# RMSNorm and matrix product: input held in two buffers of sixteen tiles instead of five of eight

## The chip, the cores and the metric

The kernel runs on one core of one Trainium2 chip. The metric is the device time of one execution in microseconds (us); "before" and "changed" below are always compared over runs on the same chip, interleaved in rounds. Times of one kernel mostly agree within some 0.5% from run to run.

## The reference

```python
batch, seq, dim, out_dim = 16, 1024, 512, 768        # x: 16384 rows of 512, float32
rms = np.sqrt(np.mean(x ** 2, axis=-1, keepdims=True) + eps)
x_norm = x / rms * gamma
return np.matmul(x_norm, weight).astype(np.float32)  # 16384 rows of 768, float32
```

The rows form 128 tiles of 128 rows. A tile of x is 256 KB, a tile of the output 384 KB; with the weights 85.5 MB must cross between memory and the core.

## The kernel before

For each pair of tiles: GpSimd casts x to bf16 (into one of four small buffers), TensorE transposes the cast tiles by words, VectorE copies the transposes out of PSUM, TensorE multiplies with the weights, ScalarE computes the squares' sums, and ScalarE (even tiles) and VectorE (odd tiles) scale the product by 1/rms into the output buffer. All loads and stores are issued by the sync engine, on one DMA queue, in program order; a load or store that must wait for its buffer or its data holds back everything behind it.

```python
G = 8
AHEAD = 28
...
xin = ctx.enter_context(tc.tile_pool(name="xin", bufs=5))      # x: 5 x 8 tiles, 16 KB per partition each
outp = ctx.enter_context(tc.tile_pool(name="out", bufs=3))     # output: 3 x 8 tiles, 24 KB per partition each
...
for j in range(2, NP):                     # j: pair of tiles 2j, 2j+1
    load_until(2 * j + AHEAD)              # issue loads whose first tile is below this
    if j + 3 < NP:
        cast(2 * j + 6, nc.gpsimd, 2)      # cast runs 3 pairs ahead
    if j + 1 < NP:
        norms(2 * j + 2, 2)                # squares run 1 pair ahead
    ...
        feed = feeder([j + 2], two)        # transposes run 2 pairs ahead, between the products
    ...
    for i, engine in ((2 * j, nc.scalar), (2 * j + 1, nc.vector)):
        a = accumulator()
        matmuls(i, a, range(K), feed)
        finish_tile(i, a, engine)          # scale; after a group's last tile: store the group
```

Of the kernel before, what the change touches and what calls it, by code (L numbers as in the profile page):

```python
# [12 lines left out]
F32 = mybir.dt.float32  # L13
BF16 = mybir.dt.bfloat16
AF = mybir.ActivationFunctionType
# [3 lines left out]
def kernel(  # L19
# [8 lines left out]
    nc = tc.nc  # L28
    P = 128

    x = x.flatten_outer_dims()
    out = out.flatten_outer_dims()
    N, D = x.shape
    _, O = out.shape
    K = D // P
    NT = N // P
    NP = NT // 2
    G = 8
    NG = NT // G
    AHEAD = 28  # L40
    WIDE = 512




    def stretches(parts):
        first, size, i = {}, {}, 0
        for g in range(NG):
            for n in parts.get(g, [G]):
                for t in range(i, i + n):  # L50
                    first[t], size[t] = i, n
                i += n
        return first, size

    opening = [1, 2, 1, 2, 2]
    x_first, x_size = stretches({0: opening, 1: [4, 4]})
    o_first, o_size = stretches({0: opening, NG - 2: [4, 4], NG - 1: [2, 2, 2, 1, 1]})

    def rows(ap, i, n):
        if i < G:  # L60
            return ap[i * P:(i + n) * P, :].rearrange("(p t) d -> p t d", t=n)
        return ap.rearrange("(g p t) d -> g p t d", p=P, t=G)[i // G, :, i % G:i % G + n, :]

    singles = ctx.enter_context(tc.tile_pool(name="singles", bufs=1))
    xin = ctx.enter_context(tc.tile_pool(name="xin", bufs=5))
    xbp = ctx.enter_context(tc.tile_pool(name="xb", bufs=4))
    junk = ctx.enter_context(tc.tile_pool(name="junk", bufs=2))
    stats = ctx.enter_context(tc.tile_pool(name="stats", bufs=4))
# [3 lines left out]
    outp = ctx.enter_context(tc.tile_pool(name="out", bufs=3))  # L72

    x_tiles, xb_tiles, tp_tiles, rstd_of, xT_tiles, o_tiles = {}, {}, {}, {}, {}, {}

    def held(tiles, i, n=1):
        return tiles[i // G][:, i % G:i % G + n, :]

    def load(i):
        if i // G not in x_tiles:  # L80
            x_tiles[i // G] = xin.tile([P, G, D], F32, name="xt")
        nc.sync.dma_start(out=held(x_tiles, i, x_size[i]), in_=rows(x, i, x_size[i]))

    starts = [i for i in range(NT) if x_first[i] == i]

    def load_until(i):
        while starts and starts[0] < i:
            load(starts.pop(0))

    def cast(i, engine, n=1):  # L90
        if i // 2 not in xb_tiles:
            xb_tiles[i // 2] = xbp.tile([P, 2, D], BF16, name="xb")
        engine.tensor_copy(out=xb_tiles[i // 2][:, i % 2:i % 2 + n, :], in_=held(x_tiles, i, n))  # L93

    def square(i, ssq):
        jk = junk.tile([P, D], BF16, name="jk")
        nc.scalar.activation(out=jk, in_=held(x_tiles, i)[:, 0, :], func=AF.Square, accum_out=ssq)  # L97

    def root(i, n, ssq):
        rms = stats.tile([P, 4], F32, name="rms")  # L100
# [29 lines left out]
    def transpose_tile(i):  # L130
        for h in range(2):
            transpose_word(i // 2, i % 2, h)
        evac(i // 2, i % 2, 1)

    def scale(engine, dst, src, r):
        if engine is nc.scalar:
            nc.scalar.mul(out=dst, in_=src, mul=r)  # L137
        else:
            nc.vector.tensor_single_scalar(out=dst, in_=src, scalar=r, op=mybir.AluOpType.mult)  # L139

    def accumulator():
        return opsum.tile([P, 2, WIDE], F32, name="ops").rearrange("p a b -> p (a b)")

    def out_tile(i):
        if i // G not in o_tiles:
            o_tiles[i // G] = outp.tile([P, G, O], F32, name="ot")
        return o_tiles[i // G][:, i % G, :]

    def store(i):
        first, n = o_first[i], o_size[i]  # L150
        if i == first + n - 1:
            nc.sync.dma_start(out=rows(out, first, n), in_=held(o_tiles, first, n))

    def matmul(i, k, acc, lo, hi):
        nc.tensor.matmul(out=acc[:, lo:hi], lhsT=xT_tiles[i // 2][:, i % 2, k // 2, :, k % 2], rhs=w_bf[:, k, lo:hi],  # L155
# [3 lines left out]
    def matmuls(i, acc, ks, feed=None):  # L159
        for k in ks:  # L160
            matmul(i, k, acc, 0, WIDE)
            if feed:
                feed()
            matmul(i, k, acc, WIDE, O)
# [20 lines left out]
    with tc.manual_schedule():  # L185
        g_row = singles.tile([2, P, 2], F32)
        nc.scalar.dma_start(out=g_row, in_=gamma.rearrange("(h w c) -> h w c", w=P, c=2))

        wv = weight.rearrange("(h w c) o -> w h (c o)", w=P, c=2)
        touched = singles.tile([P, 2, 1], F32)  # L190
        nc.scalar.dma_start(out=touched, in_=wv[:, :, 0:1])
        nc.scalar.preload_act_table(AF.Sqrt)  # L192
        load_until(3)
        w_f32 = singles.tile([P, K, O], F32)
        for h in range(2):
            nc.sync.dma_start(out=w_f32[:, 2 * h:2 * h + 2, :].rearrange("p c o -> p (c o)"), in_=wv[:, h, :])
        load_until(AHEAD)


        warm = singles.tile([P, WIDE], BF16)  # L200
        nc.vector.memset(warm, 0.0)  # L201
        eps_sb = singles.tile([P, 1], F32)
        nc.vector.memset(eps_sb, float(eps))  # L203
        ident_f = singles.tile([P, P], F32)
        make_identity(nc, ident_f)
        spare = accumulator()

        def warm_up(n):
            for _ in range(n):
                nc.tensor.matmul(out=spare[:, :WIDE], lhsT=warm[:, :P], rhs=warm, start=True, stop=True)  # L210

        w_bf = singles.tile([P, K, O], BF16)

        def weights(k, engine, lo=0, hi=O):
            scale(engine, w_bf[:, k, lo:hi], w_f32[:, k, lo:hi], g_sb[:, k % 2, k // 2:k // 2 + 1])


        ssq = stats.tile([P, 4], F32, name="ssq")
        warm_up(6)
        cast(0, nc.vector)  # L220
        square(0, ssq[:, 0:1])
        gp = tpsum.tile([P, 2, 2], F32, name="tp")
        for c in range(2):
            nc.tensor.transpose(out=gp[:, c, :], in_=g_row[:, :, c], identity=ident_f[:2, :2])  # L224
        g_sb = singles.tile([P, 2, 2], F32)
        nc.vector.tensor_copy(out=g_sb, in_=gp)
        transpose_tile(0)
        warm_up(3)
        cast(1, nc.vector)
        cast(2, nc.gpsimd)  # L230
        square(1, ssq[:, 1:2])
        square(2, ssq[:, 2:3])
        transpose_tile(1)
        transpose_tile(2)
        warm_up(2)

        acc = [accumulator() for _ in range(4)]
        weights(0, nc.vector, 0, WIDE)
        weights(0, nc.vector, WIDE, O)
        weights(1, nc.scalar)  # L240
        for k in (0, 1):
            for i in range(3):
                matmuls(i, acc[i], [k])
        root(0, 3, ssq)
        weights(2, nc.vector)
        weights(3, nc.scalar)
        cast(3, nc.gpsimd)
        matmuls(0, acc[0], [2, 3])
        finish_tile(0, acc[0], nc.scalar)
        transpose_tile(3)  # L250
        norms(3, 1)
        matmuls(1, acc[1], [2, 3])
        finish_tile(1, acc[1], nc.vector)
        cast(4, nc.gpsimd)
        cast(5, nc.gpsimd)
        matmuls(2, acc[2], [2, 3])
        finish_tile(2, acc[2], nc.scalar)
        matmuls(3, acc[3], [0, 1, 2, 3], feeder([2], [0, 2, 2, 0], alone=True))
        finish_tile(3, acc[3], nc.vector)
        cast(6, nc.gpsimd, 2)  # L260
        cast(8, nc.gpsimd, 2)
        norms(4, 2)


        one, two, both = [1, 1, 0, 1, 1, 0, 0, 0], [1, 0, 1, 0, 1, 0, 1, 0], [1, 1, 1, 1, 1, 1, 1, 1]
        for j in range(2, NP):
            load_until(2 * j + AHEAD)
            if j + 3 < NP:
                cast(2 * j + 6, nc.gpsimd, 2)
            if j + 1 < NP:  # L270
                norms(2 * j + 2, 2)
            if j == NP - 1:
                break
            if j < 4:
                feed = feeder([j + 1], one)
            elif j == 4:
                feed = feeder([5, 6], both)
            elif j + 2 < NP:
                feed = feeder([j + 2], two)
            else:  # L280
                feed = None
# [3 lines that stand above are left out]
                finish_tile(i, a, engine)  # L285


        for i in (NT - 2, NT - 1):
            for lo, hi, engine in ((0, WIDE, nc.scalar), (WIDE, O, nc.vector)):
                a = accumulator()  # L290
                for k in range(K):
                    matmul(i, k, a, lo, hi)
                scale(engine, out_tile(i)[:, lo:hi], a[:, lo:hi], rstd_of[i])
            store(i)
# [35 lines left out]
```

## Time and profile before

| what | before |
|---|---|
| time, median | 210.9 us |
| span in the profile | 209.0 us |
| TensorE busy | 95% of the span |
| DMA queue busy | 97% of the span |
| one period (8 tiles): TensorE / DMA | 12.15 / 12.25 us |
| issue to landing: store of 3 MiB / load of 2 MiB, issued at 46 us | 20.2 / 24.6 us |

How to read it: a high busy share of DMA engines says that transfers stood in the queue, not that anyone waited for them. What binds is read from who waits for whom, and from how the time from issue to landing changes along the run. The prediction below shows these lines and reads them.

### The profile page before, as it was taken

The numbers are of one execution on the slowest core, as the hardware profiler recorded it, in microseconds if no ns is written. First come the engines' busy times: TensorE is split into PE (matmuls) and PEld (weight loads), VectorE is DVE, ScalarE is ACT, GpSimd is POOL, SyncE is SP. The second block draws the span as 40 slices with busy tenths as digits, with TensorE's granted clock in tenths as the row PEclk, the third lists the DMA queues.
The fourth block names the chain that finished last, engine by engine and source line by source line (L and its number), as shares of the span: only waits on it lengthen the run. The fifth ranks groups of instructions, "written<-read, shape, count | busy, mean of one in ns | idle before, by whom it ended". The sixth has DMA issues, their size and how long they took to land.

```text
span 209.0 us, 3555 instructions
## 1 busy us (share of the span) xinstructions
PE 198.7 (95%) x1268; PEld 137.5 (66%) x1293; DVE 111.6 (53%) x204; ACT 158.3 (76%) x388; POOL 66.4 (32%) x71
## 2 busy tenths in 40 slices
PE   7899999999999999999999999999999999999960
PEld 3466776667666776677666766676666766776630
DVE  2566565466456545644654565466456545645630
ACT  4599678778877877887787778778777877887830
POOL 1165443233323323332332333233223323310000
PEclk9999999999999999999999999999999999999997
DMA  6999999999999999999999999999999999998983
GB/s 223 413 426 444 396 404 422 423 448 411 433 426 417 455 415 442 408 439 415 423 448 415 445 408 448 430 415 444 408 444 423 434 437 426 409 423 357 412 347 142
DMA packets 7206, 85.69 MB, mean 410 GB/s; under 512 B 1042, under 2 KB 1044, under 8 KB 3220
## 3 DMA queue, kind: packets, MB, share of 16 engines
q1 hardware_dynamic: 6912, 85.46, 97.0%
q8 instruction: 10, 0.16, 0.3%
q10 hardware_dynamic: 276, 0.00, 0.1%
q14 instruction: 8, 0.07, 0.1%
HBM read 35.13 MB, written 50.33 MB: 409 GB/s over the span
## 4 chain that ended last, share of the span: by engine, by line
PE 93%; DVE 2%; issue 1%; ACT 1%
PE ops L155 78%; PE tp L120 13%; PE ops L210 1%; DVE ot L139 1%; DVE xT L127 1%; ACT ot L137 0%; ACT jk L97 0%; DVE xb L93 0%; DVE w_bf L139 0%; PE tp L224 0%; ACT rms L101 0%; DVE warm L201 0%; DVE rstd L103 0%; DVE eps_sb L203 0%
## 5 line engine op out<-in xcount | busy, mean ns | idle before, releaser
L155 PE MATMUL ops<-w_bf,xT 128*128 128x512 bf16 (+1 forms) x999 | 192.5, 324 | 1.9 <-DVE w_bf L139 0.6
L155 PEld LDWEIGHTS <-xT 128*128 128x128 bf16 x1024 | 100.2, 98 | 57.0 <-issue 1.0
L93 POOL CAST xb<-xt 128x1024 bf16<-128x1024 f32 (+1 forms) x65 | 65.7, 1016 | 118.5 <-PE tp L120 108.1
L127 DVE COPY xT<-tp 128x1024 bf16<-128x1024 bf16 (+1 forms) x67 | 44.5, 667 | 80.8 <-PE tp L120 80.8
L137 ACT ACTIVATE ot<-ops,rstd 128x768 f32<-128x768 f32 (+1 forms) x65 | 58.1, 894 | 37.7 <-PE ops L155 36.9
L97 ACT ACTIVATE jk<-xt 128x512 bf16<-128x512 f32 x128 | 78.8, 619 | 1.2 <-DMA xt<-in_x_dram 1.2
L120 PE MATMUL tp<-ident_f,xb 128*128 128x128 f32 x256 | 69.0, 274 | 0.3 <-DVE xb L93 0.2
L139 DVE TENSOR_SCALAR ot<-ops,rstd 128x768 f32<-128x768 f32 (+1 forms) x65 | 64.5, 992 | 2.9 <-PE ops L155 2.8
L120 PEld LDWEIGHTS tp<-ident_f,xb 128*128 128x128 f32 x256 | 35.9, 141 | 3.8 <-issue 0.8
L97 ACT ACTIVATION_READ_ACCUMULATOR jk<-xt 128x1 f32 x128 | 24.4, 190 | 0.0
L101 ACT ACTIVATE rms<-ssq,eps_sb 128x2 f32<-128x2 f32 (+1 forms) x64 | 18.9, 295 | 2.0
L103 DVE RECIPROCAL rstd<-rms 128x2 f32<-128x2 f32 (+1 forms) x64 | 9.9, 155 | 3.2 <-ACT rms L101 3.1
L210 PE MATMUL ops<-warm 128*128 128x512 bf16 x11 | 4.5, 555 | 1.2 <-DVE eps_sb L203 1.2
L210 PEld LDWEIGHTS <-warm 128*128 128x128 bf16 x11 | 1.4, 134 | 2.6 <-issue 1.4
L137 ACT ACTIVATE w_bf<-w_f,g_sb 128x768 bf16<-128x768 f32 x2 | 1.9, 936 | 1.4 <-DMA w_f<-in_weight_dram 0.7
L192 ACT ACT_TABLE_LOAD x1 | 1.3, 1283 | 1.8 <-issue 1.8
L93 DVE CAST xb<-xt 128x512 bf16<-128x512 f32 x2 | 1.1, 530 | 2.5 <-DMA xt<-in_x_dram 2.5
L139 DVE TENSOR_SCALAR w_bf<-w_f,g_sb 128x512 bf16<-128x512 f32 (+2 forms) x3 | 1.4, 480 | 0.5 <-DMA w_f<-in_weight_dram 0.5
L224 PEld LDWEIGHTS tp<-ident_f,g_row 2*128 2x128 f32 x2 | 0.3, 200 | 0.8 <-issue 0.8
L201 DVE MEMSET warm<- 128x256 uint32 x1 | 0.3, 272 | 0.9 <-PEq L311 0.9
L224 PE MATMUL tp<-ident_f,g_row 2*128 2x2 f32 x2 | 0.4, 264 | 0.0
masks.py:199 POOL TENSOR_SCALAR_AFFINE_SELECT ident_f<-ident_f 128x128 f32<-128x128 f32 x1 | 0.3, 294 | 0.1
(7 smaller groups left out, 0.8 us busy)
## 6 DMA issues: line engine op xcount, KB each, us to landing
out_dram<-ot SPq DMA_DIRECT2D x13, 3072.0 KB, 20.5
xt<-in_x_dram SPq DMA_DIRECT2D x14, 2048.0 KB, 24.9
out_dram<-ot SPq DMA_DIRECT2D x6, 768.0 KB, 7.0
out_dram<-ot SPq DMA_DIRECT2D x2, 1536.0 KB, 9.0
xt<-in_x_dram SPq DMA_DIRECT2D x2, 1024.0 KB, 11.1
xt<-in_x_dram SPq DMA_DIRECT2D x3, 512.0 KB, 5.7
w_f<-in_weight_dram SPq DMA_DIRECT2D x2, 768.0 KB, 6.0
out_dram<-ot SPq DMA_DIRECT2D x4, 384.0 KB, 17.9
```

Source lines behind the costliest of these rows:

```text
L93: engine.tensor_copy(out=xb_tiles[i // 2][:, i % 2:i % 2 + n, :], in_=held(x_tiles, i, n))
L97: nc.scalar.activation(out=jk, in_=held(x_tiles, i)[:, 0, :], func=AF.Square, accum_out=ssq)
L101: nc.scalar.activation(out=rms[:, :n], in_=ssq[:, :n], func=AF.Sqrt, scale=1.0 / D, bias=eps_sb)
L103: nc.vector.reciprocal(out=rstd[:, :n], in_=rms[:, :n])
L120: nc.tensor.transpose(out=tp_tiles[j][:, t, h, :], in_=words[:, lo:lo + P], identity=ident_f)
L127: nc.vector.tensor_copy(out=dst[:, t:t + n, :], in_=src[:, t:t + n, :])
L137: nc.scalar.mul(out=dst, in_=src, mul=r)
L139: nc.vector.tensor_single_scalar(out=dst, in_=src, scalar=r, op=mybir.AluOpType.mult)
L155: nc.tensor.matmul(out=acc[:, lo:hi], lhsT=xT_tiles[i // 2][:, i % 2, k // 2, :, k % 2], rhs=w_bf[:, k, lo:hi], start=(k == 0), stop=(k == ...
L192: nc.scalar.preload_act_table(AF.Sqrt)
L210: nc.tensor.matmul(out=spare[:, :WIDE], lhsT=warm[:, :P], rhs=warm, start=True, stop=True)
L224: nc.tensor.transpose(out=gp[:, c, :], in_=g_row[:, :, c], identity=ident_f[:2, :2])
```

## The change

The intent: half as many, twice as large loads in the steady part (32 KB in one piece per partition), and 64 KB instead of 80 KB of each partition for x. The output keeps its buffers of eight tiles.

```diff
-    G = 8
-    NG = NT // G
-    AHEAD = 28
+    XG, OG = 16, 8
+    AHEAD = 20
...
-    x_first, x_size = stretches({0: opening, 1: [4, 4]})
-    o_first, o_size = stretches({0: opening, NG - 2: [4, 4], NG - 1: [2, 2, 2, 1, 1]})
+    last = NT // OG - 1
+    x_first, x_size = stretches(XG, {0: opening + [4, 4], 1: [4, 4, 8]})
+    o_first, o_size = stretches(OG, {0: opening, 1: [4, 4], last - 1: [4, 4], last: [2, 2, 2, 1, 1]})
...
-        return ap.rearrange("(g p t) d -> g p t d", p=P, t=G)[i // G, :, i % G:i % G + n, :]
+        return ap.rearrange("(g p t) d -> g p t d", p=P, t=XG)[i // XG, :, i % XG:i % XG + n, :]
...
-    xin = ctx.enter_context(tc.tile_pool(name="xin", bufs=5))
+    xin = ctx.enter_context(tc.tile_pool(name="xin", bufs=2))
...
-        load_until(AHEAD)
+        load_until(2 * XG)
```

(The helpers take the group size as an argument, and the first sixteen tiles, not eight, are laid out piece by piece.) The order of the sync queue in the steady part, a load of 16 tiles and two stores of 8 in each period of 16 tiles, becomes:

```
store 24..31   store 32..39   load 64..79   store 40..47   store 48..55   load 80..95
```

More of the change, by code (lines that the diff above doesn't have):

```diff
@@ L37, with stretches @@
     NP = NT // 2
-    G = 8
-    NG = NT // G
-    AHEAD = 28
+    XG, OG = 16, 8
+    AHEAD = 20
     WIDE = 512
-    def stretches(parts):
+    def stretches(group, parts):
         first, size, i = {}, {}, 0
-        for g in range(NG):
-            for n in parts.get(g, [G]):
+        for g in range(NT // group):
+            for n in parts.get(g, [group]):
                 for t in range(i, i + n):
@@ L55 @@
     opening = [1, 2, 1, 2, 2]
-    x_first, x_size = stretches({0: opening, 1: [4, 4]})
-    o_first, o_size = stretches({0: opening, NG - 2: [4, 4], NG - 1: [2, 2, 2, 1, 1]})
+    last = NT // OG - 1
+    x_first, x_size = stretches(XG, {0: opening + [4, 4], 1: [4, 4, 8]})
+    o_first, o_size = stretches(OG, {0: opening, 1: [4, 4], last - 1: [4, 4], last: [2, 2, 2, 1, 1]})
     def rows(ap, i, n):
-        if i < G:
+        if i < XG:
             return ap[i * P:(i + n) * P, :].rearrange("(p t) d -> p t d", t=n)
-        return ap.rearrange("(g p t) d -> g p t d", p=P, t=G)[i // G, :, i % G:i % G + n, :]
+        return ap.rearrange("(g p t) d -> g p t d", p=P, t=XG)[i // XG, :, i % XG:i % XG + n, :]
     singles = ctx.enter_context(tc.tile_pool(name="singles", bufs=1))
-    xin = ctx.enter_context(tc.tile_pool(name="xin", bufs=5))
+    xin = ctx.enter_context(tc.tile_pool(name="xin", bufs=2))
     xbp = ctx.enter_context(tc.tile_pool(name="xb", bufs=4))
@@ L74, with held @@
     x_tiles, xb_tiles, tp_tiles, rstd_of, xT_tiles, o_tiles = {}, {}, {}, {}, {}, {}
-    def held(tiles, i, n=1):
-        return tiles[i // G][:, i % G:i % G + n, :]
+    def held(tiles, group, i, n=1):
+        return tiles[i // group][:, i % group:i % group + n, :]
     def load(i):
-        if i // G not in x_tiles:
-            x_tiles[i // G] = xin.tile([P, G, D], F32, name="xt")
-        nc.sync.dma_start(out=held(x_tiles, i, x_size[i]), in_=rows(x, i, x_size[i]))
+        if i // XG not in x_tiles:
+            x_tiles[i // XG] = xin.tile([P, XG, D], F32, name="xt")
+        nc.sync.dma_start(out=held(x_tiles, XG, i, x_size[i]), in_=rows(x, i, x_size[i]))
     starts = [i for i in range(NT) if x_first[i] == i]
@@ L92, in cast @@
             xb_tiles[i // 2] = xbp.tile([P, 2, D], BF16, name="xb")
-        engine.tensor_copy(out=xb_tiles[i // 2][:, i % 2:i % 2 + n, :], in_=held(x_tiles, i, n))
+        engine.tensor_copy(out=xb_tiles[i // 2][:, i % 2:i % 2 + n, :], in_=held(x_tiles, XG, i, n))
     def square(i, ssq):
         jk = junk.tile([P, D], BF16, name="jk")
-        nc.scalar.activation(out=jk, in_=held(x_tiles, i)[:, 0, :], func=AF.Square, accum_out=ssq)
+        nc.scalar.activation(out=jk, in_=held(x_tiles, XG, i)[:, 0, :], func=AF.Square, accum_out=ssq)
     def root(i, n, ssq):
@@ L144, in out_tile @@
     def out_tile(i):
-        if i // G not in o_tiles:
-            o_tiles[i // G] = outp.tile([P, G, O], F32, name="ot")
-        return o_tiles[i // G][:, i % G, :]
+        if i // OG not in o_tiles:
+            o_tiles[i // OG] = outp.tile([P, OG, O], F32, name="ot")
+        return o_tiles[i // OG][:, i % OG, :]
     def store(i):
@@ L151, in store @@
         if i == first + n - 1:
-            nc.sync.dma_start(out=rows(out, first, n), in_=held(o_tiles, first, n))
+            nc.sync.dma_start(out=rows(out, first, n), in_=held(o_tiles, OG, first, n))
     def matmul(i, k, acc, lo, hi):
```

## The prediction

> **What bounds the kernel now.** I read the page first: busy shares, then the chain that ended last.
>
> ```profile
> PE 198.7 (95%) x1268; PEld 137.5 (66%) x1293; DVE 111.6 (53%) x204; ACT 158.3 (76%) x388; POOL 66.4 (32%) x71
> q1 hardware_dynamic: 6912, 85.46, 97.0%
> PE 93%; DVE 2%; issue 1%; ACT 1%
> ```
>
> TensorE is 95% busy and carries 93% of the chain, yet the one DMA queue (q1: packets, MB, share of 16 engines) is busy 97%. Two resources are near full, so I need to know which one sets the pace. The queue's timeline shows the beat (start us, us, engine, line):
>
> ```profile
> 34.17 0.33 SPq L152 DMA_DIRECT2D out_dram<-ot  x1
> 34.60 0.75 SPq L82 DMA_DIRECT2D xt<-in_x_dram  x1
> 46.32 0.33 SPq L152 DMA_DIRECT2D out_dram<-ot  x1
> 46.75 0.70 SPq L82 DMA_DIRECT2D xt<-in_x_dram  x1
> 58.47 0.33 SPq L152 DMA_DIRECT2D out_dram<-ot  x1
> ```
>
> Every 12.15 us one store of 3 MiB and one load of 2 MiB go out: eight tiles, 1.52 us a tile. The wait view says who sets this beat:
>
> ```profile
> POOL xb L93 <- DMA xt<-in_x_dram: 9.8, 4, 3.9
> SPq L152 <- DVE ot L139: 168.6, 23, 11.8
> ```
>
> The queue waits 168.6 us for scaled results; compute waits for loads only in the opening (four waits of GpSimd, its last at 14.7 us in the timeline). So **TensorE paces the steady part**. How far is DMA behind? The issue view restricted to short windows gives single latencies (last column: us from issue to landing). The windows are at 34, 46 and 143 us; in each a store, then its load:
>
> ```profile
> out_dram<-ot SPq DMA_DIRECT2D x1, 3072.0 KB, 19.6
> xt<-in_x_dram SPq DMA_DIRECT2D x1, 2048.0 KB, 24.6
> ...
> out_dram<-ot SPq DMA_DIRECT2D x1, 3072.0 KB, 20.2
> xt<-in_x_dram SPq DMA_DIRECT2D x1, 2048.0 KB, 24.6
> ...
> out_dram<-ot SPq DMA_DIRECT2D x1, 3072.0 KB, 21.1
> xt<-in_x_dram SPq DMA_DIRECT2D x1, 2048.0 KB, 25.5
> ```
>
> Adding latency to issue: the store at 46.32 lands at 66.5, its load at 71.4, 4.9 us later; the next store to land takes about 7.3. So the queue is served in order, at 2.097 MB / 4.9 = 428 GB/s for loads and 3.146 / 7.3 = 431 for stores. The load issued at 34.6 landed at 59.2, that of 143.9 at 169.4: nine periods of 12.25 us against TensorE's 12.15. DMA is thus 0.1 us a period slower than compute, and lives on a backlog of some 20 us of queued work. It catches up when the loads have ended, after 169 us: store latency falls from 21.1 to 5.4 us, and DMA's share drops to 0.47 in the slice 192 to 193 us, its queue empty for a moment. The end, too, is then TensorE's. A change to transfers gains only if it removes a TensorE wait, and loses if it makes one.
>
> **What the Trainium skill says.** "DMA: Bandwidth & Descriptors", section "Anatomy of one DMA", gives one transfer about 2 us of fixed cost plus its bytes at 436 GB/s, the fixed part mostly the receipt at the end. The trace agrees: the first load (256 KB) takes 2.9 us issue to landing, while back to back transfers land 4.9 us per 2 MiB, so the fixed part overlaps in a full queue. The same page, "Queues, rings and completion order", says that descriptors of a queue are consumed in ring order on each engine; the landing chain above agrees. "Why small descriptors are slow" there puts a penalty of a few cycles on each packet, which is 27% at 256 bytes. Rows here are 16 and 24 KB already, so 32 KB rows should gain nothing visible. "HBM Reference", section "Access", has about 425 GB/s for a core streaming alone; the trace has 426 to 429 in the stretches 34 to 83 and 83 to 144 us. There is no headroom of bandwidth to win.
>
> **The change part by part.**
> 1. *Instructions.* The order comparison shows the same instructions in the same order on TensorE, VectorE, ScalarE and GpSimd; only the sync queue differs. 12 loads of 2 MiB there become 6 of 4 MiB; tiles 16 to 31 come in 4, 4 and 8; the store of tiles 8 to 15 is split in two. Issuing costs 0.3 to 1.0 us each on an engine that idles: zero on the path. Bytes are unchanged.
> 2. *Buffers.* x goes from 5x8 = 40 tiles to 2x16 = 32. Load g (tiles 16g to 16g+15) can go only when load g-2 has been read to its last tile. The last reader is ScalarE's square of tile 16g-17; it runs in the iteration of tile 16g-20, so it ends about 0.7 us into that tile. The first reader of the new load is GpSimd's cast of tiles 16g, 16g+1; TensorE transposes those during tile 16g-4. Distance: 16 tiles x 1.52 = 24.3 us, less 0.7 of the square and 1.04 of the cast (its row: 1042 ns): some 22.5 us for a load that needs 9.75 us of DMA by itself (2 x 4.87), plus what stands before it.
> 3. *The first such load (tiles 32 to 47).* Square 15 ends near 27.5 us, and the order has the load behind the store of tiles 8 to 11, possible at 28.1 (tile 15's scaling starts at 33.10, four tiles earlier is 27.03, plus 1.01). So issue at about 28.5. Landings before: load of tiles 32 to 39 at 18.60 + 21.1 = 39.7; take its 4.87 away, as it is no longer there, and the store ahead of it landed near 34.9. Store of tiles 6, 7 (1.9 us): 36.8. Store of tiles 8 to 11 (1.57 MB, 3.7 us): 40.5. The 4 MiB load: 9.75, **landing 50.3**. Needed: the first transpose of tile 32 starts its weight load at 50.95 in the trace before (tile 28's stretch), less 1.04 for the cast: **49.9**. TensorE stalls about **0.5 us**.
>
> ```profile
> 50.95 0.14 PEld L120 LDWEIGHTS tp<-ident_f,xb 128*128 128x128 f32 x1
> ```
>
> 4. *Later loads.* Tiles 48 to 63: behind the load (50.3) land the stores of tiles 12 to 15 (3.7) and 16 to 23 (7.3): 61.3; the load issued at 52 lands at 71.1, needed at 49.9 + 24.3 = 74.2. Slack 3.1 us. Each further period of 16 tiles takes DMA 24.5 against TensorE's 24.3, so the slack shrinks 0.2 a period, to some 2.3 at the sixth load. No stall. Output buffers: a store issued at the end of a group must land before the group three later writes, two group times = 24.3 us; latency some 20, as before. No stall.
> 5. *Tail.* Stores have the same sizes; total DMA work is unchanged and never starved until 192 us. TensorE ends 0.5 later, and the end moves with it.
> Sum: 210.9 + 0.5 = **211.4 us**.
>
> **The rivals.**
> *A, the load wait is larger.* Step 3 compares two times near 50 us; each DMA estimate carries perhaps 1 us, and the part stores of the opening are slow (365 and 377 GB/s in 24 to 28 us). The first load could be 2 or 3 us late; TensorE pays that once, for later loads shift with it and keep their slack. Result 212 to 214.
> *B, DMA becomes the bound through its layout.* An output store of eight tiles now writes 24 KB pieces at a pitch of 48 KB, not one solid block. If that costs 3% of bandwidth, the slack of step 4 is used up within five periods and DMA's whole stream sets the end: 214 to 217. Against it: the tail already writes 12 KB pieces at 24 KB pitch, 1.57 MB landing 3.8 us apart, which is 414 GB/s with a transfer boundary in it.
> *C, fewer and larger transfers are faster.* 428 GB/s against the peak slices of 440 to 448 leaves 3% at most; but DMA is not what TensorE waits for in the steady part, and the queue already runs empty at 192 us, so a gain is hidden. Result 210.5 to 211. For over 2% faster, 4 us would have to vanish from a 95% busy TensorE whose instructions are the same.
> *D, the sync queue blocks.* A load waiting for its buffer holds back later stores, as the queue issues in order. But the wait ends at tile 28 of its period, the next store comes at tile 32. Each issue also waits for the transfer eight issues back to land (that held the load at 23.59 in the trace before). In the opening the 8-tile load then waits until about 8.9 us for the second weight transfer, not 6.9, with some 11 us of DMA work queued: harmless.
>
> **Range and chances.** Centre 211.4. The low end is no stall at all, with the usual scatter: 210.5. The high end, 213.2, is a first load 2.3 us late, or a small loss of bandwidth. Slower by over 2% (215.1) needs B, or A beyond 4 us: 5%. Faster by over 2%: 1%.
>
> **What would show it.** Step 1: the same instruction counts, 6 loads of 4096 KB in the issue view. Steps 2 and 3: in the wait view GpSimd's cast waits once more on the load, near 50 us, and TensorE idles some 0.5 us for the cast there; the load's latency is 22 us. Step 4: later loads land in about 19 us, at a steady 24.3 us beat, with no TensorE wait. Step 5: DMA share still 97%. It is wrong if the load waits recur each period (A or B), if GB/s in the steady stretch leaves 420 to 435, or if a store's buffer wait shows on ScalarE or VectorE.

## The result, and the profile after

The changed kernel takes 210.78 us (median of six runs, 210.38 to 211.36), the kernel before 210.86 us (six runs, 210.72 to 211.21). The ratio is 0.9995, with a 95% interval of 0.9976 to 1.0014. (A ratio is the mean time of one kernel's fast runs over that of the other's of the same rounds, so not quite the ratio of the medians quoted.) No difference.

The page of the changed kernel: busy shares, the queue, and the shares of the chain that ended last. TensorE and DMA stand where they stood; the queue has fewer packets for the same megabytes. The 3% of DMA in the chain are the arrival of the weights in the opening.

```profile
PE 199.0 (95%) x1268; PEld 137.7 (66%) x1293; DVE 111.6 (54%) x204; ACT 158.2 (76%) x388; POOL 65.8 (32%) x71
q1 hardware_dynamic: 6336, 85.46, 97.0%
PE 91%; DMA 3%; DVE 1%; ACT 1%; issue 1%; SPq 0%; DVEq 0%
```

Its sync queue in order of time (start us, us, engine, line, what, how many):

```profile
29.53 1.14 SPq L83 DMA_DIRECT2D xt<-in_x_dram  x1
...
52.81 0.34 SPq L83 DMA_DIRECT2D xt<-in_x_dram  x1
59.46 12.48 SPq L153 DMA_DIRECT2D out_dram<-ot  x2
...
83.76 12.49 SPq L153 DMA_DIRECT2D out_dram<-ot  x2
```

The beat is 83.76 - 59.46 = 24.30 us for 16 tiles, which is 12.15 for eight: TensorE's pace of before, to the hundredth. Its waits (engine and line, for whom: us in total, times, longest):

```profile
POOL xb L94 <- DMA xt<-in_x_dram: 55.3, 11, 9.7
...
PEld tp L121 <- POOL xb L94: 0.2, 1, 0.2
```

The timeline has the place of the last one:

```profile
11.29 0.20 PEld L121 LDWEIGHTS tp<-ident_f,xb 128*128 128x128 f32 x2 [0.20 <-POOL xb L94]
```

GpSimd now waits 55.3 us for loads, up from 9.8, and once for 9.7 us. The line of TensorE's weight load (PEld) is what counts: TensorE waited for a cast once, for 0.2 us, and that was at 11.3 us, in the opening. Of the waits for the 4 MiB loads nothing reached it. GpSimd has a lead of three pairs, and uses it up. The two loads issued at 29.53 and 52.81 us (last column: us to landing):

```profile
xt<-in_x_dram SPq DMA_DIRECT2D x1, 4096.0 KB, 20.7
xt<-in_x_dram SPq DMA_DIRECT2D x1, 4096.0 KB, 18.4
```

They land at 50.2 and 71.2 us (start plus latency). Rates in the steady stretch (busy time of each engine with the number of instructions, granted clock, DMA share, GB/s), before and then changed:

```profile
83.00:144.00 61.00, 60.58 (x395) 42.77 (x402) 33.74 (x60) 48.59 (x121) 20.84 (x20) 1.00 1.01 429
```

```profile
83.00:144.00 61.00, 60.58 (x394) 42.77 (x402) 34.02 (x61) 48.58 (x123) 18.76 (x19) 1.00 1.00 429
```

429 GB/s in both: rows of 32 KB move no faster than rows of 16 KB, and the pieces of 24 KB at a pitch of 48 KB in the output no slower.

Two things did not follow the prediction, and they cancel. First, TensorE's first product. Before, then changed:

```profile
7.68 2.81 PE L155 MATMUL ops<-w_bf,xT 128*128 128x512 bf16 x16 [0.59 <-DVE w_bf L139]
```

```profile
8.67 2.81 PE L156 MATMUL ops<-w_bf,xT 128*128 128x512 bf16 x16 [1.43 <-DVE w_bf L140]
```

The changed kernel began its products 1.0 us late, since its weights landed later, and stayed 1.0 us late to its last store (issued at 203.7 us against 202.7). Second, that last store. Before, then changed:

```profile
out_dram<-ot SPq DMA_DIRECT2D x1, 384.0 KB, 5.4
```

```profile
out_dram<-ot SPq DMA_DIRECT2D x1, 384.0 KB, 4.0
```

It lands 1.4 us sooner after its issue. So the spans are 209.0 and 208.6 us. The experiments ask whether the change has anything to do with either, and how close the new loads really are to TensorE's need.

### The profile page after: what moved, and what is told of

Read it like the earlier page. It is cut to its first block, busy times and chain, and to the rows that moved or that the text cites. A ratio compares the mean times of both kernels' runs of the same rounds, so it can differ in the third digit from the quotient of the medians.

```text
span 208.6 us, 3553 instructions
## 1 busy us (share of the span) xinstructions
PE 199.0 (95%) x1268; PEld 137.7 (66%) x1293; DVE 111.6 (54%) x204; ACT 158.2 (76%) x388; POOL 65.8 (32%) x71
## 4 chain that ended last, share of the span: by engine, by line
PE 91%; DMA 3%; DVE 1%; ACT 1%; issue 1%; SPq 0%; DVEq 0%
PE ops L156 78%; PE tp L121 13%; DMA w_f<-in_weight_dram 3%; DVE ot L140 1%; ACT ot L138 0%; SPq L83 0%; ACT jk L98 0%; DVE w_bf L140 0%; DVE xT L128 0%; ACT rms L102 0%; DVE rstd L104 0%; DVEq L140 0%
```

## The experiments

My theory after the result: every load has a deadline in TensorE's work, and every store one in the reuse of the three output buffers. The one queue serves both in order. The changed kernel meets all deadlines, so it costs nothing; and nobody was waiting for DMA before, so it gains nothing. A small lateness of TensorE is absorbed at the end, because the last stores stand behind others in the queue. (So at the very end the kernel does wait for DMA; e3 and e4 bear on this.) Rivals: the loads have slack to spare and the buffers hardly matter; or the larger transfers gain something that is lost elsewhere.

Eleven runs were made, one of them (e9) of the changed kernel itself, all with correct results. They ran in three calls on different chips; each is compared with runs of the kernel before from its own call (medians 211.22, 211.22 and 211.03 us).

### e1: every load two tiles later

```diff
-    AHEAD = 20
+    AHEAD = 18
```

This moves each 4 MiB load by one step in the queue: it now stands behind the store of the eight tiles that have just been finished, instead of ahead of it.

> The changed kernel with the load of 16 tiles issued one iteration (two tiles) later, so that it stands behind the next store of the sync queue. Theory (loads have 1.5 to 4 us of slack and no more): the first 4 MiB load now lands behind the store of tiles 12 to 15, near 54.0 us (40.5 + 3.7 + 9.75) and is needed at 49.9 to 50.9; TensorE stalls 3 to 4 us there, then some 0.2 us a period because the DMA chain takes 24.5 us against 24.3. The tail gives about 1.4 us back. Time 213 to 215 us. Rival (the loads have slack to spare and TensorE alone sets the time): 210.8 us, GpSimd waits longer but TensorE does not.

Measured: 255.06 us, ratio 1.2058 (1.2016 to 1.2101). The direction was the theory's; the size was wrong by a factor of over ten. Its wait view and the DMA row of its page (40 slices, busy share in tenths):

```profile
PEld tp L121 <- POOL xb L94: 35.4, 7, 6.8
```

```profile
DMA  7999999992599957999349996198990999939896
```

Six of the seven waits are at the 4 MiB loads (the seventh, 0.2 us, is in the opening): TensorE now waits for the cast in every period. The expectation had DMA always at work. The row shows that it isn't: once a period a slice falls far below 9. The windows of the first such gap (columns as above) tell why it is so dear:

```profile
40.00:50.00 10.00, 9.95 (x67) 7.01 (x66) 5.32 (x11) 7.61 (x19) 0.00 (x0) 1.00 1.07 450
50.00:56.00 6.00, 1.44 (x10) 0.73 (x8) 1.69 (x3) 2.06 (x6) 1.20 (x2) 0.78 0.94 395
56.00:60.00 4.00, 3.78 (x13) 2.23 (x15) 0.00 (x0) 1.24 (x2) 2.80 (x3) 0.50 0.57 246
60.00:66.00 6.00, 6.00 (x39) 4.24 (x39) 3.38 (x6) 3.96 (x12) 2.08 (x2) 0.98 0.02 7
```

The load lands at 54.7 us (54.0 expected), and from 51 to 56 us TensorE waits for it. When it may go on, at 56 us, it has a granted clock (the share of full clock pulses that it is given) of 0.50 for some 4 us. By then the queue has finished all it was given: from 60 to 66 us it moves 7 GB/s. The next thing in the queue is a store whose tiles TensorE has yet to compute, and the next load stands behind it. So the next load begins with an empty queue, must wait for 3 MiB of store, and is late again. TensorE's row of waits and its busy time account for the loss: 32.9 us idle for the cast and 212.0 - 199.0 = 13.0 us more busy at the low clock, against 253.6 - 208.6 = 45.0 us more span. The half clock agrees with the Trainium skill, "TensorE: Matmul & The Clock Gate", section "HAM oscillation", which warns of idle gaps above about 3.4 us: the waits here were 5 to 6.8 us. The limit itself does not come out of these runs: TensorE was idle from 51.3 us, and its clock was already 0.69 in 53 to 54 us and 0.50 in 54 to 55; e5 shows the half clock after a gap of 2.7 us.

### e2: each load in two halves, back to back

```diff
-        nc.sync.dma_start(out=held(x_tiles, XG, i, x_size[i]), in_=rows(x, i, x_size[i]))
+        n = x_size[i] if i < 2 * XG else 8
+        for h in range(i, i + x_size[i], n):
+            nc.sync.dma_start(out=held(x_tiles, XG, h, n), in_=rows(x, h, n))
```

> The changed kernel with each 4 MiB load split into two of 2 MiB issued back to back: only the transfer size changes. Theory (size of a transfer does not matter at 16 or 32 KB rows): 210.8 us within 0.5, the steady stretch moves 426 to 430 GB/s, GpSimd's longest wait for a load falls by about 4.9 us as the first half lands earlier. Rival (large loads speed DMA up and the gain is hidden or used at the tail): under 426 GB/s in the stretch 34 to 144 us, the landing of the last load later by over 1 us, last store's latency back from 4.0 to 5.4 us.

Measured: 211.19 us, ratio 1.0001 (0.9965 to 1.0037); 427 and 430 GB/s in the stretches 34 to 83 and 83 to 144 us, against 429 and 429 of the changed kernel. The longest wait of GpSimd for a load fell from 9.7 to 5.3 us, 4.4 of the 4.9 expected. The size of the transfer does not show in the rate. The latency of the last store, 4.3 us, stayed near 4.0.

### e3 and e4: the kernel before, with TensorE started late

```diff
-        warm_up(2)            # the last of three calls
+        warm_up(8)            # e3; in e4: warm_up(14)
```

> The kernel before with six more warm-up matmuls ahead of the first product, so that TensorE starts its work 0.7 to 1.2 us later (read from the trace). Theory (the last stores of the kernel before still stand in a DMA backlog of 1.4 us, 5.4 us latency against 4.0, so a late start of TensorE is absorbed): 210.9 to 211.2 us, last store's latency falls to 4.0 to 4.7. Rival (the end is TensorE's, as the prediction said): 211.6 to 212.1 us, latency stays 5.4.

> The same with twelve more warm-up matmuls: TensorE starts 2 to 3 us later. Theory (1.4 us are absorbed, the rest shows): 211.5 to 212.6 us, last store's latency at its floor of 4.0 us. Rival (the end is TensorE's): 212.9 to 213.9 us. Rival (DMA's stream alone sets the end): 210.9 us.

Measured: 211.01 us, ratio 0.9983 (0.9959 to 1.0007), and 211.28 us, ratio 0.9994 (0.9970 to 1.0018). The first product of e4, and its last store:

```profile
9.76 2.76 PE L155 MATMUL ops<-w_bf,xT 128*128 128x512 bf16 x16
```

```profile
out_dram<-ot SPq DMA_DIRECT2D x1, 384.0 KB, 4.0
```

In e3 TensorE begins 0.5 us later than in the kernel before, less than planned, and the last store takes 5.1 us. In e4 it begins 2.1 us later and issues its last store 2.0 later, yet the time stays: the interval is -0.6 to +0.4 us. That is below the theory's 211.5 to 212.6 us. The rival that DMA's stream alone sets the end (210.9) comes closest, and the prediction's view, that the end is TensorE's (212.9 or more), falls.

The theory failed on its floor of 4.0 us. There is no such floor: the last store of e6 took 3.1 us and that of e1 3.5. In e4 the queue was still catching up at the end, for the last two stores (768 KB) landed within 1.9 us of the one before them, though issued 2.1 us after it. The traced execution of e4, the slowest of its six, has a span 0.7 us longer; its last load had landed at 170.1 instead of 169.4 us, so most of the 0.7 is older than the tail. Nearly all of the 2.0 us is thus free. The end of the kernel before is set by the DMA queue, which is still behind, and not by TensorE.

### e5: only the first 4 MiB load late

```diff
-            load_until(2 * j + AHEAD)
+            load_until(2 * j + (18 if j < 9 else AHEAD))
```

> The changed kernel with only its first 4 MiB load issued two tiles later, behind the store of tiles 12 to 15; the other five loads keep their place. Theory (a late load costs TensorE once; in the run with all loads late the stalls recurred because there each load waits for the store of its own period, so the queue runs dry): the load lands near 54.7 us as in that run, TensorE stalls 4 to 5 us once, no further wait, the queue never runs dry; last product about 4 us later than 202 us, tail latency 4.0 us, so 213.9 to 214.9 us. Rival (a stall breeds the next, whatever the order): stalls at each period and over 230 us.

Measured: 216.04 us, 215.01 to 217.11, ratio 1.0235 (1.0184 to 1.0286). TensorE's wait for the cast in the profiled run (215.01 us):

```profile
PE tp L121 <- POOL xb L94: 2.7, 1, 2.7
```

It waits once, and the rest of the run has the usual beat: the stall does not breed others, and the rival falls. The time missed the expectation by 0.1 to 2.2 us. The wait is shorter than the 4 to 5 us expected, as TensorE had started 1.2 us late (8.90 instead of 7.68). But after the stall its clock was 0.83 in 54 to 56 us, 0.50 in 56 to 58 and 0.82 in 58 to 60, which the expectation left out. An estimate from these: 2 x (0.17 + 0.50 + 0.18) = 1.7 us lost. The other runs were not traced; the two near 217 us also have the lower mean clock (0.984 and 0.983, against 0.990 and 0.989).

### e6: three buffers of sixteen tiles

```diff
-    AHEAD = 20
+    AHEAD = 36
...
-    xin = ctx.enter_context(tc.tile_pool(name="xin", bufs=2))
+    xin = ctx.enter_context(tc.tile_pool(name="xin", bufs=3))
```

> The changed kernel with three buffers of sixteen tiles and loads issued sixteen tiles earlier: size of a load as in the changed kernel, more read ahead than either. Theory (beyond a slack of a few us more read ahead only lengthens the queue): 210.5 to 211.3 us; GpSimd waits for loads in the opening only, under 20 us in all; loads take 25 us or more to land, stores over 20. Rival (read ahead is worth something): faster by over 1 us.

Measured: 215.76 us, 214.49 to 216.41, ratio 1.0214 (1.0174 to 1.0254). Both theories missed: more read ahead is slower. Its wait view has a new line, and the store issued at 58.5 us shows the reason (us to landing):

```profile
ACT ot L138 <- DMA out_dram<-ot: 8.2, 2, 6.9
```

```profile
out_dram<-ot SPq DMA_DIRECT2D x1, 3072.0 KB, 30.7
```

The additional load goes into the queue ahead of the stores and pushes them back. A store must land within 24.3 us, when its output buffer is due for reuse; this one took 30.7. ScalarE waited 6.9 us to write its result, TensorE stood idle for 4.3 us of it, and its clock was 0.50 in 66 to 70 us. That is the other deadline of my theory, and I had not worked it out for this run.

### e7: the kernel before with four buffers

```diff
-    xin = ctx.enter_context(tc.tile_pool(name="xin", bufs=5))
+    xin = ctx.enter_context(tc.tile_pool(name="xin", bufs=4))
```

> The kernel before with four instead of five buffers of eight tiles: read ahead cut to 32 tiles as in the changed kernel, size of a load unchanged. Theory (32 tiles in small loads still leave over 10 us of slack): 210.6 to 211.3 us, no wait of GpSimd for loads after the opening, loads land in less than 25 us. Rival (the loss of read ahead costs and the larger size pays it back in the changed kernel): 212 us or more.

Measured: 211.17 us, ratio 1.0002 (0.9979 to 1.0026). The read ahead of 32 tiles, taken alone, costs nothing. Who waits is now the sync queue, for ScalarE to leave a buffer (the queue's own waits), and that harms nobody:

```profile
SPq L82 <- ACT jk L97: 56.8, 11, 5.7
```

With e2 this takes the change apart: neither the size of the loads nor the read ahead moves the time by itself. (The new opening was not varied by itself.)

### e8 and e10: loads ahead of the stores, with three and with four output buffers

```diff
-    AHEAD = 20
+    AHEAD = 28            # e8 and e10
...
-    outp = ctx.enter_context(tc.tile_pool(name="out", bufs=3))
+    outp = ctx.enter_context(tc.tile_pool(name="out", bufs=4))      # e10 alone
```

Here each load stands one store earlier in the queue than in the changed kernel. Its buffer is not free yet, so it blocks the queue.

> The changed kernel with each load placed before the store of the preceding eight tiles in the sync queue: the load waits at the head of the queue for its buffer and holds the store back by some 6 us. Theory (the queue then nearly runs dry while the store waits, so DMA loses up to 1 us a period, but loads land 7 us earlier against their need): no TensorE wait for a load, DMA share in the stretch 34 to 144 us at 0.95 to 1.0, 211 to 213.5 us. Rival (order of the queue does not matter while TensorE does not wait): 210.8 us. Rival (a blocked store fills the output buffers and stops ScalarE and VectorE): over 215 us with waits of the scaling on stores.

> The run with loads ahead of the stores, with four output buffers instead of three. Theory (its 221 us come from stores that land after the three output buffers are all full): no or little wait of the scaling on stores, 211 to 214 us. Rival (the DMA queue loses the time itself, running dry while the queue's head waits for a buffer): over 217 us, with the waits of the scaling gone and waits for loads in their place.

Measured: e8 221.33 us, ratio 1.0508 (1.0463 to 1.0552); e10 213.72 us, ratio 1.0125 (1.0082 to 1.0169). The wait view of e8:

```profile
ACT ot L138 <- DMA out_dram<-ot: 18.9, 5, 4.8
```

In e8 my theory (211 to 213.5 us) missed and the second rival holds: stores come too late for three output buffers. e10 takes that wait away with a fourth buffer, and 7.6 us of the time go with it (the two ran on different chips, whose kernels before differ by 0.2 us). What is left in e10 is not a wait of TensorE. Its window from 34 to 83 us, and its last store:

```profile
34.00:83.00 49.00, 49.00 (x325) 34.36 (x323) 27.41 (x50) 39.09 (x98) 17.00 (x17) 1.00 0.95 388
```

```profile
out_dram<-ot SPq DMA_DIRECT2D x1, 384.0 KB, 8.3
```

TensorE is busy 49.00 of 49.00 us, but DMA moved only 388 GB/s there, as the blocked queue ran short (share of 0.57 and 0.48 in 50 to 52 and 52 to 54 us; the load could go at 52.9). At the changed kernel's 429 GB/s the same bytes need 49 x 388 / 429 = 44.3 us, so 4.7 us of DMA time were lost. They came back at the end as a longer queue: the last store took 8.3 us instead of 4.0. The span is 4.4 us longer than the changed kernel's.

### e9: the changed kernel once more

> The changed kernel once more, unaltered, for a second trace. The weights landed 1.1 us later in the changed kernel's trace than in the one of before, with the same transfers ahead of them. Theory (that is scatter from one execution to the next): over the traces the arrival of the first weights (8.0 us in the changed kernel's first trace, 6.95 before) takes values from 6.8 to 8.3 in both kernels; time 210.4 to 211.4 us. If this trace starts early, the first load's landing near 50.4 meets TensorE's need and a wait of up to 0.6 us shows. Rival (the change delays the weights): first weights at 7.9 to 8.3 us again.

Measured: 210.62 us, ratio 0.9975 (0.9942 to 1.0007), and a profiled run in which TensorE's first product began at 7.62 us, not 8.67. The first weights landed 5.2 us after their issue (6.4 in the first trace of this kernel, 5.3 before): with the same kernel they come early or late, so the change does not always delay them. Over all thirteen traces the time ran from 5.2 to 6.6 us. But it was above 6 in four of the nine traces with the changed opening and in none of the four with the old one (at most 5.8). Whether the new opening makes a late arrival more frequent is not shown. With the early opening the stall of the prediction's third step appears. GpSimd's cast after the first 4 MiB load, and TensorE's weight load behind it:

```profile
50.99 3.01 POOL L94 CAST xb<-xt 128x1024 bf16<-128x1024 f32 x3 [11.34 <-DMA xt<-in_x_dram]
...
52.08 0.14 PEld L121 LDWEIGHTS tp<-ident_f,xb 128*128 128x128 f32 x1 [1.20 <-POOL xb L94]
```

TensorE's weight load waits 1.2 us. In the first trace the same cast began at 50.38 us and TensorE, 1.0 us late from its opening, did not wait. After that the two executions run alike: the store goes out at 59.44 and at 59.46 us. In one the opening had cost the 1.0 us, in the other the load's landing took it back. The span is 209.0 us, as before the change, since the last store again took less than before (4.4 us): TensorE's 1.0 us is absorbed, as in e4.

### e11: every load two tiles later, in halves

The edits of e1 and e2 together.

> The run with all loads two tiles later (255 us), with each load in two halves of 2 MiB. Theory (a whole load lands 4.9 us after its first half would, and its first tile waits for the whole): each of six stalls shrinks by 4.9 us, so 255 less 29 = 226 us, within 5. Rival (only the order in the queue counts, not the size of the load): 250 us or more.

Measured: 215.12 us, ratio 1.0183 (1.0135 to 1.0231). The theory had the direction, but expected 226. Its wait of TensorE for the cast:

```profile
PEld tp L123 <- POOL xb L96: 5.2, 6, 1.7
```

The waits of TensorE are at most 1.7 us long. No clock below 1.00 shows in the windows from 50 to 64 us, where e1 had 0.50, and DMA's share from 34 to 190 us is 1.00 on average (413 GB/s), where e1's queue ran dry. Taking 4.9 us from each wait of e1 thus also removed most of what followed from each. My expectation subtracted the first and forgot the second.

## Why the prediction was right or wrong

The time, 210.78 us, lies in the range, and "within 2%" was the likely outcome. Step by step:

1. *Instructions.* Right. The beat of 24.30 us and the rate of 429 GB/s show no cost and no gain of larger transfers (e2 confirms it). The Trainium skill's 425 GB/s for a core streaming alone ("HBM Reference") stand in its section "Specifications (TRN2)"; the traces have 426 to 429.
2. *Buffers.* Right as a mechanism. e1 shows that the distance of 22.5 us worked out there has little to spare: behind one store more the load misses TensorE in each period.
3. *The first load.* Landing predicted at 50.3, measured 50.2 and 50.8 us in the two traces. The stall predicted at 0.5 us was absent in the trace with a late opening, and 1.2 with the early one that the step had assumed. The mechanism is right, the size within 0.7 us. The term that was too small is the load itself: it landed 10.3 us after the store ahead of it in both traces, not 9.75. Whether there is a stall at all depends on when the weights land, which varies by 1 us from one execution to the next.
4. *Later loads.* Right: latencies of 18.4 to 19.3 us for "about 19", landing of the second at 71.2 for 71.1, no wait of TensorE.
5. *The tail.* Wrong. "TensorE ends 0.5 later, and the end moves with it" failed: TensorE ended 1.0 later in both traces and the end did not move. I had taken one slice with a share of 0.47 for proof that the queue was empty at 192 us. It was not: the store issued at 186.0 us landed at 196.1. What the runs show instead is that the queue sets the end. From the landing of the last 3 MiB store to that of the last store it took 15.6 us before, 15.7 changed and 15.5 in e4, whose TensorE was 2.0 us late; in e5, whose stall had let the queue catch up, it took 17.8. e10 is the opposite case, in which TensorE never waits for a 4 MiB load and the end moves by DMA's loss alone. Without the 0.5 us of stall carried to the end, the sum would have been 210.9, against 210.78 measured. The range held in spite of this step, because its term was only 0.5 us.

Of the rivals, C said that a gain would be hidden; no gain was seen at all, and as the queue sets the end, one could have shown there. (C's "3% at most" is also too small: the page's highest slice is 455 GB/s, 6% above 428.) B's loss by the layout of the output did not occur (429 GB/s in the same stretch). In A, the 365 and 377 GB/s of 24 to 28 us are read wrongly: between the landings at 23.5 and 29.3 us the queue moved a load of 2 MiB, not the stores. A's claim that a late load costs once was right for a single load (e5), and wrong as soon as each load stands behind its period's store (e1): there each stall empties the queue and prepares the next. D called a blocked queue harmless on the grounds of where the load stands, and that holds only there: one store earlier it costs 10 us (e8).

What stays open: why the spread of e5 was wide, why the weights' arrival varies, and whether the new opening has a part in it.

## What to carry to other kernels

Where one queue carries loads and stores and both DMA and the computing engine are near full, count two deadlines: the load against its first reader, and the store against the reuse of its output buffer. Moving a transfer by one place in the queue can break either, and the loss can be more than ten times what the distance suggests (e1), because a stalled producer also leaves the queue without work. Reading ahead further is not safer by itself: it pushes the stores back. To see what the end of a kernel depends on, see whether the last stores land closer together than they were issued, and start the computing engine late on purpose.

## What the Trainium skill lacked or had wrong

- "DMA: Bandwidth & Descriptors", "Anatomy of one DMA — SWDGE (gpsimd) path", fits 2.0 us plus the bytes at 436 GB/s to transfers that GpSimd issues. Those here are issued by the sync engine: the first load of 256 KB took 2.6 to 2.9 us in the thirteen traces (2.6 by that sum). The page gives no separate figure for stores: the shortest last store of 384 KB took 3.1 us (e6; 2.9 by that sum).
- "Trainium Kernel Development and Optimization", "Best Practices", recommends double buffering for overlap. No page that I read says that a load blocked at the head of a queue which also carries stores can cost more than it hides: 221.33 us against 211.22 in e8, and that further read ahead can do the same (215.76 us in e6).
- "TensorE: Matmul & The Clock Gate", "HAM oscillation", has about 3.4 us as the idle gap to stay below. These runs saw a clock of 0.50 after shorter ones: 2.7 us in e5, and 2.1 us in e8 (idle from 152.5 to 154.6 us, clock 0.50 in 156 to 158), while another gap of 2.15 us in e8 (from 99.6 us) and the waits of up to 1.7 us in e11 left it at 1.00.
